# Expert weights in 2 MB loads of 16 KB per partition, in a transformer-block kernel on one Trainium2 core

## The chip, the core and the metric

The kernel runs on one core of a Trainium2 chip. Its engines are TensorE (PE; PEld is its weight load), VectorE (DVE), ScalarE (ACT), GpSimd (POOL) and SyncE (SP), which issues nearly all DMAs; 16 DMA engines carry the bytes. Each engine runs its own instructions in the order in which they stand, and a semaphore holds an instruction back until what it needs is there. The metric is the time of one execution on the device, in microseconds (us): the median of three runs before the change is 1225.87 us.

## What is computed

One layer on 256 tokens of width 1024, float32, with 16 meta tokens ahead of them. The first part mixes a gated attention branch and a state-space (S5) branch; the second part is a mixture of 32 experts, and all 32 experts' weights are read:

```python
h = layer_norm(concat([meta, x]), ln_in_g, ln_in_b)
proj = h @ w_in                      # q, k, v, forget gate, u, and two gates g_a, g_b
y_a = forgetting_attention(q, k, v, log_f)
y_b = gelu(s5_ssm(u, ...)); y_b = y_b * sigmoid(y_b @ w_glu + b_glu)
mix = (sigmoid(g_a) * (y_a @ w_up_a) + sigmoid(g_b) * (y_b @ w_up_b)) @ w_o
h = layer_norm(ALPHA * h + mix, ln1_g, ln1_b)
top_v, top_i = top_k(h @ w_router + b_router, 4); top_w = softmax(top_v)
for e in range(32):
    gate = minimum(h @ w_gate[e] + b_gate[e], 7); up = clip(h @ w_up[e] + b_up[e], -7, 7)
    out += comb[:, e] * (((up + 1) * gate * sigmoid(1.702 * gate)) @ w_down[e] + b_down[e])
h = layer_norm(ALPHA * h + out, ln2_g, ln2_b)
```

Each expert has three matrices of 1024 x 1024 float32, 4 MB each: 384 MB in all.

## The kernel before

**Slots.** Weights live in slots of 8 KB per partition (1 MB over 128 partitions). Three pools hold them: `wA` (6 slots, open from the start), `wC` (5, in memory that the attention part frees) and `wB` (7, in memory that the scan part frees). Three tiles of the same size serve as further slots when their first use is over: `gate1` and `acc` in the pool `keep`, `hT` in `fk`. In the first part `wA` takes the slabs of `w_in`, `w_up_a`, `w_glu` and `w_up_b` (`slab`), two slots to a slab, and `wB` the four quarters of `w_o`.

**Expert loads.** `expert_load(w, e, qtr)` loads a quarter of an expert's matrix, 256 rows: partition p gets the rows 2p and 2p+1, so that one run of 8192 bytes goes to a partition. `home` lists the slot of each load in order: 21 loads find a slot without waiting for an expert (`first`); after that the slots come round again, 20 of them, later 19. `prefetch` issues the first 21 loads between the steps of the first part, in the order gate, up of expert 0, gate, up of expert 1, then down.

**Order.** SP and PE run in the order in which the code is written (`manual_schedule`); in most of the kernel the instructions of DVE, ACT and POOL are put in an order by a list scheduler, which moves an instruction ahead where its inputs are expected early. SP's DMAs use eight semaphores in turn, so an issue also waits until the DMA eight places earlier has landed, and everything behind a waiting issue waits with it.

**First part.** `u_tile`, `k_tile`, `q_tile`, `v_tile` and `gate_tile` are projections on PE (`project`, L214). Between them stand the scan (`scan_b`, `scan_u`, `scan_out`), whose tables `E` DVE builds by doubling (L419 to L422), and the attention (`scores`, `values`). `wr` (router weights) and `brow` are loaded behind the slab `wv`; from them POOL makes `wrg` (L675, L677) and DVE reduces `wsum` (L676, L678, L679). `braw` holds the gate and up biases; ACT casts it to `bias` (L834, L838), and POOL subtracts in between (L837).

**Experts.** The 32 experts run in pairs p. `gate_up` multiplies the pair's gathered tokens (64 per expert) with gate and up, two matmuls of 512 columns for each of the eight k, `activate` and `act_T` make and transpose the activations, `gather` collects the next pair's tokens, and `down` goes through the down matrices of both experts together. The last pair is taken expert by expert (`down_one`). As a partition holds the rows 2p and 2p+1, k stands for every second column within 256: `paired(k)` takes these columns of `z1` and of the activations, and `affine` the matching norm parameters from `pcolP`.

Of the kernel before, what the change touches and what calls it, by code (L numbers as in the profile page):

```python
# [33 lines left out]
NWA, NWB, NWC = 6, 7, 5  # L34
# [14 lines left out]
def hybrid_trunk_kernel(ctx: ExitStack, tc: tile.TileContext, x, meta, ln_in_g, ln_in_b, w_in, b_f,  # L49
# [44 lines left out]
    prowP = sp.tile([8, 256], F32, name="prowP")  # L94
    ldt = sp.tile([16, 2], F32, name="ldt")

    def slab(src, kt):

        n = src.shape[1]
        src = src.rearrange("(k p) n -> p k n", p=P)  # L100
        nk, ks = 2048 // n, []
        for k0 in range(0, kt, nk):
            v_ = wA.tile([P, 2048], F32, name="w", tag="w").rearrange("p (k n) -> p k n", n=n)
            nc.sync.dma_start(v_, src[:, k0:k0 + nk])
            ks += [v_[:, k] for k in range(nk)]
        return ks
# [21 lines left out]
    for j, a in enumerate((ln1_g, ln1_b)):  # L128
        nc.sync.dma_start(prowP[4 * j:4 * j + 4], a.rearrange("l (q n) -> (l q) n", n=256))
# [140 lines left out]
    for k in range(2):  # L270
        TE.transpose(pp[:, 8 * k:8 * k + 8], prowP[:, k::2], ident[:8, :8])
# [424 lines left out]
    slots = [("wC", "w")] * NWC + [("wB", "w")] * (NWB - 4) + [("wA", "w")] * NWA + [("keep", "gate1")]  # L696
    slots += [("wB", "w")] * 4 + [("fk", "hT")]
    first = slots[:NWC + NWB + NWA - 3] + [("keep", "acc")] + slots[NWC + NWB + NWA - 3:]

    def homes():  # L700

        out = list(first)
        while len(out) <= 12 * NE:
            out += [s_ for s_ in slots if s_ != ("keep", "gate1") or len(out) < 9 * NE - 24]
        return out[:12 * NE + 1]
# [14 lines left out]
    def expert_load(w, e, qtr, load=True):  # L720
        key = (w.tensor.name, e, qtr)
        if key in ready:
            return ready.pop(key)
        pool, tag = home[nload[0]]
        nload[0] += 1
        t_ = pools[pool].tile([P, 2048], F32, name="w", tag=tag).rearrange("p (k n) -> p k n", n=D)
        if load:
            nc.sync.dma_start(t_, w[0, e, qtr * 256:qtr * 256 + 256].rearrange("(p k) n -> p k n", k=2))
        return t_

    def prefetch(n):
        seq = [(w, e, qtr) for e in range(2) for w in (w_gate, w_up) for qtr in range(4)]
        seq += [(w_down, e, qtr) for qtr in range(4) for e in range(2)]
        for _ in range(n):
            w, e, qtr = seq[nload[0]]
            ready[(w.tensor.name, e, qtr)] = expert_load(w, e, qtr)

    prefetch(2)
# [20 lines left out]
    prefetch(2)  # L759
# [39 lines left out]
    prefetch(NWB - 4)  # L799
# [74 lines left out]
    def paired(k):  # L874

        return slice(256 * (k // 2) + k % 2, 256 * (k // 2) + 256, 2)

    def affine(k, out_, in_, natural=False):
        if natural:
            g_, b_ = col(R_L1G + k), col(R_L1B + k)  # L880
        else:
            c = 8 * (k % 2) + k // 2
            g_, b_ = pcolP[:, c:c + 1], pcolP[:, c + 4:c + 5]
# [471 lines left out]
```

## Time and profile before

| | before |
|---|---|
| runs, median (lowest to highest) | 1225.87 us (1224.28 to 1227.44) |
| the profiled execution: its time, and the span from first to last instruction | 1222.52 us, 1221.0 us |
| busy: PE, PEld, DVE, ACT, POOL | 1124.1, 588.9, 340.4, 177.3, 71.6 us |
| DMA | 433.60 MB in 75674 packets, 355 GB/s over the span |
| chain of work that ended last | DMA 53%, PE 38%, DVE 5% |

PE's busy time counts pipelined matmuls whose ends are modelled, so 92% doesn't mean that PE sets the time. The chain is followed back from the last instruction; where it reads DMA, an instruction was waiting for a load. The trace gives, for each engine, every instruction with its start and duration and what ended its idle time, and for the DMA engines bytes, packets and the share of time in which they were busy.

### The profile page before, as it was taken

The page shows a single profiled execution, that of the slowest core. Times are in us where ns is not written, and L with a number is a line of the kernel's source. Part 1 is how long each engine was busy: PE and PEld are TensorE (multiplying, and loading weights), DVE is VectorE, ACT ScalarE, POOL GpSimd, SP SyncE. Part 2 cuts the span into 40 slices and gives each one's busy share as a digit, 9 for nine tenths or more (in the row PEclk, how much of TensorE's full clock was granted, in tenths as well). Part 3 has the DMA queues.
Part 4 walks back from the last instruction along what each step waited for, and adds up shares of the span by engine and source line. Part 5 has one row for each costly group of instructions (what it writes and reads, how often), then busy time and mean ns, then how long its engine had stood idle before and what let it go on. Part 6 is the DMA issues. An engine that isn't in the chain of part 4 may idle for free.

```text
span 1221.0 us, 13200 instructions
## 1 busy us (share of the span) xinstructions
PE 1124.1 (92%) x5398; PEld 588.9 (48%) x5399; DVE 340.4 (28%) x782; ACT 177.3 (15%) x387; POOL 71.6 (6%) x118
## 2 busy tenths in 40 slices
PE   4889999998999999999999999998999899998994
PEld 2777788754545444444434363535433343443331
DVE  3969420533221212112131312130212121202013
ACT  2357410311101011010101010101010111101000
POOL 3333200400000000000000000000000000000001
PEclk9999999998999999999999999999999999999998
DMA  7742289557999999999999999999999999999992
GB/s 150 187 105 69 104 211 357 221 208 301 413 422 420 423 420 421 422 420 407 421 422 422 421 422 421 421 421 419 422 420 422 421 421 421 421 421 420 422 421 104
DMA packets 75674, 433.60 MB, mean 355 GB/s; under 512 B 14218, under 2 KB 14570, under 8 KB 26586
## 3 DMA queue, kind: packets, MB, share of 16 engines
q1 hardware_dynamic: 75178, 432.19, 89.3%
q8 instruction: 44, 0.72, 0.2%
q10 hardware_dynamic: 432, 0.52, 0.1%
q14 instruction: 20, 0.16, 0.0%
HBM read 431.64 MB, written 1.05 MB: 354 GB/s over the span
## 4 chain that ended last, share of the span: by engine, by line
DMA 53%; PE 38%; DVE 5%; ACT 1%; issue 1%; POOL 1%; SPq 1%; POOLq 0%; ACTq 0%; DVEq 0%
DMA w<-in_w_up_dram 29%; DMA w<-in_w_down_dram 16%; PE ps L214 7%; PE pu L1062 6%; PE pg L1062 6%; PE Yp L1094 5%; DMA w<-in_w_gate_dram 5%; PE ps L764 2%; PE px L945 2%; DMA w<-in_b_down_dram 2%; PE Yp L1108 1%; PE ps L936 1%; PE po L936 1%; PE px L1124 1%; DMA prow<-in_ssm_a_im_dram 1%
## 5 line engine op out<-in xcount | busy, mean ns | idle before, releaser
L1062 PE MATMUL pu<-w,xy 128*64 128x512 f32 x1024 | 238.5, 595 | 13.5 <-DMA w<-in_w_up_dram 13.5
L1062 PE MATMUL pg<-w,xy 128*64 128x512 f32 x1024 | 236.9, 594 | 3.3 <-PEq L1153 2.1
L1094 PE MATMUL Yp<-w,aT 128*64 128x512 f32 x960 | 228.1, 611 | 0.0
L1094 PEld LDWEIGHTS Yp<-w,aT 128*64 128x64 f32 x960 | 101.5, 141 | 114.7 <-issue 99.1
L1062 PEld LDWEIGHTS pu<-w,xy 128*64 128x64 f32 x1024 | 81.4, 136 | 154.8 <-issue 108.9
L1062 PEld LDWEIGHTS pg<-w,xy 128*64 128x64 f32 x1024 | 86.6, 137 | 140.4 <-issue 134.0
L214 PE MATMUL ps<-hT,w 128*128 128x256 f32 (+1 forms) x512 | 119.3, 392 | 2.8 <-ACT pr L595 2.8
L214 PEld LDWEIGHTS ps<-hT,w 128*128 128x128 f32 x512 | 98.0, 194 | 19.7 <-ACT pr L595 3.1
L1072 DVE TENSOR_SCALAR pg<-pg 128x512 f32<-128x512 f32 x32 | 22.4, 699 | 232.7 <-PE pg L1065 232.7
L1073 ACT ACTIVATE ups<-pg 128x512 f32<-128x512 f32 x32 | 19.1, 597 | 415.3 <-DVE pg L1072 415.3
L1075 DVE TENSOR_SCALAR pu<-pu 128x512 f32<-128x512 f32 x32 | 22.4, 700 | 186.8 <-PE pu L1065 186.8
L1097 DVE COPY xy<-Yp 128x512 f32<-128x512 f32 x15 | 10.4, 692 | 223.3 <-PE Yp L1094 223.3
L1124 PE MATMUL px<-xy,selT 128*128 128x512 f32 x120 | 61.7, 636 | 4.7 <-DVE acc L1126 2.6
L945 PE MATMUL px<-sel,z 128*128 128x128 f32 x480 | 59.8, 283 | 0.6 <-DVE sel L950 0.6
L1313 POOL TENSOR_TENSOR acc<-acc,gb 128x512 f32<-128x512 f32 (+1 forms) x2 | 2.4, 1214 | 979.6 <-ACT acc L1311 979.6
L945 PEld LDWEIGHTS px<-sel,z 128*128 128x128 f32 x480 | 58.6, 196 | 0.8 <-ACT aT L1084 0.8
L1124 PEld LDWEIGHTS px<-xy,selT 128*128 128x128 f32 x120 | 20.4, 193 | 42.3 <-DVE acc L1126 19.2
L1126 DVE TENSOR_TENSOR acc<-acc,px 128x512 f32<-128x512 f32 x56 | 37.3, 683 | 12.3 <-PE px L1124 12.2
L1098 ACT COPY xy<-Yp 128x512 f32<-128x512 f32 x15 | 8.8, 586 | 218.3 <-PE Yp L1094 218.3
L1084 ACT COPY aT<-px 128x512 f32<-128x512 f32 x32 | 18.8, 586 | 133.6 <-PE px L1082 133.6
L885 DVE TENSOR_SCALAR xy<-px,pcolP 128x128 f32<-128x128 f32 x60 | 23.7, 410 | 45.4 <-ACT xy L887 43.4
L887 ACT ACTIVATE xy<-px,pcolP 128x128 f32<-128x128 f32 x60 | 25.8, 455 | 44.6 <-PE px L945 42.6
(399 smaller groups left out, 838.2 us busy)
## 6 DMA issues: line engine op xcount, KB each, us to landing
w<-in_w_gate_dram SPq DMA_DIRECT2D x128, 1024.0 KB
w<-in_w_up_dram SPq DMA_DIRECT2D x128, 1024.0 KB
w<-in_w_down_dram SPq DMA_DIRECT2D x127, 1024.0 KB
w<-in_w_in_dram SPq DMA_DIRECT2D x16, 1024.0 KB
w<-in_w_o_dram SPq DMA_DIRECT2D x4, 1024.0 KB
w<-in_w_up_a_dram SPq DMA_DIRECT2D x2, 1024.0 KB
w<-in_w_up_b_dram SPq DMA_DIRECT2D x2, 1024.0 KB
w<-in_w_glu_dram SPq DMA_DIRECT2D x1, 1024.0 KB
```

The source lines that it names most:

```text
L214: TE.matmul(pt, w[k][:, j * P:(j + 1) * P], hT[:, k, n0:n1], start=k == 0, stop=k == KD - 1)
L764: TE.matmul(pt, w[k][:, d * P:(d + 1) * P], y[:, k], start=k == 0, stop=k == 3)
L885: V.tensor_scalar(out_, in_, g_, b_, op0=ALU.mult, op1=ALU.add)
L887: S.activation(out_, in_, AF.Identity, scale=g_, bias=b_)
L936: TE.matmul(po[i][n], mT[:, k, i * P:(i + 1) * P], wo[k // 2][:, k % 2, n * 512:n * 512 + 512], start=False, stop=k == KD - 1, skip_group_ ...
L945: TE.matmul(pts[k // 4][:, (k % 4) * P:(k % 4 + 1) * P], z1[:, i, paired(k)], sel[:, i].rearrange("p e s -> p (e s)"), start=i == 0 and k ...
L1062: TE.matmul(pt[64 * n:64 * n + 64], XT[:, kk, c0:c0 + CAP], wt[:, k, n * 512:n * 512 + 512], start=kk == 0, stop=False, skip_group_check=True)
L1072: V.tensor_scalar_min(pgt, pgt, 7.0)
L1075: V.tensor_scalar(put, put, 7.0, -7.0, op0=ALU.min, op1=ALU.max)
L1094: TE.matmul(Yp[n][64 * g:64 * g + 64], aTs[g][:, j, half], wd[g][:, k, n * 512:n * 512 + 512], start=qtr == 0 and k == 0, stop=qtr == 3 an ...
L1124: TE.matmul(pt, selT[:, i * P:(i + 1) * P], Ysb[:, ns], start=True, stop=True)
L1126: V.tensor_add(acc[:, i, ns], acc[:, i, ns], pt)
```

## The change

An expert load is now half a matrix, 512 rows or 2 MB: partition p gets four neighbouring rows, 4p to 4p+3, one run of 16384 bytes. The slots are 16 KB per partition: 4 in `wA`, 3 in `wB`, 2 in `wC`. A load into the small tiles takes two of them (`PAIR`: `gate1` and `hT`; in the first round `acc` and `gate1`) and is issued as two DMAs of 1 MB. The first round has 10 loads (20 MB); after that the places come round, 10 of them, later 9. The slabs of the first part use the same slots, one slab to a slot, still in DMAs of 1 MB. The very last load is issued in two DMAs. `paired(k)` now steps by four columns, `prowP` has four rows and shares the tile `etmp` of the scan tables, and `down` goes through a half of each expert at a time. `crowded` handles the case that an expert has more than 64 tokens.

```diff
-NWA, NWB, NWC = 6, 7, 5
+NWA, NWB, NWC = 4, 3, 2
...
-    prowP = sp.tile([8, 256], F32, name="prowP")
+    prowP = sp.tile([P, 512], F32, name="prowP", tag="etmp")[:4]
...
-        nk, ks = 2048 // n, []
+        nk = 2048 // n
+        v_ = wA.tile([P, 4096], F32, name="w", tag="w").rearrange("p (k n) -> p k n", n=n)
         for k0 in range(0, kt, nk):
-            v_ = wA.tile([P, 2048], F32, name="w", tag="w").rearrange("p (k n) -> p k n", n=n)
-            nc.sync.dma_start(v_, src[:, k0:k0 + nk])
-            ks += [v_[:, k] for k in range(nk)]
-        return ks
+            nc.sync.dma_start(v_[:, k0:k0 + nk], src[:, k0:k0 + nk])
+        return [v_[:, k] for k in range(kt)]
...
-    slots = [("wC", "w")] * NWC + [("wB", "w")] * (NWB - 4) + [("wA", "w")] * NWA + [("keep", "gate1")]
-    slots += [("wB", "w")] * 4 + [("fk", "hT")]
-    first = slots[:NWC + NWB + NWA - 3] + [("keep", "acc")] + slots[NWC + NWB + NWA - 3:]
+    PAIR = (("keep", "gate1"), ("fk", "hT"))
+    slots = [(("wC", "w"),)] * NWC + [(("wB", "w"),)] * (NWB - 2) + [(("wA", "w"),)] * NWA + [PAIR]
+    slots += [(("wB", "w"),)] * 2
+    first = slots[:NWC + NWB + NWA - 2] + [(("keep", "acc"), ("keep", "gate1"))] + slots[-2:]
...
+    def part_load(t_, w, e, hf_, k0, nk):
+        nc.sync.dma_start(t_, w[0, e, 512 * hf_:512 * hf_ + 512].rearrange("(p k) n -> p k n", k=4)[:, k0:k0 + nk])
...
+        place = home[nload[0]]
         nload[0] += 1
+        ks = []
+        for pool, tag in place:
+            n = 4 // len(place)
+            t_ = pools[pool].tile([P, n * D], F32, name="w", tag=tag).rearrange("p (k n) -> p k n", n=D)
+            for k0 in range(0, n, nk):
+                part_load(t_[:, k0:k0 + min(n, nk)], w, e, hf_, len(ks) + k0, min(n, nk))
+            ks += [t_[:, k] for k in range(n)]
+        return ks
...
-    prefetch(2)
+    prefetch(1)
...
-    prefetch(NWB - 4)
+    prefetch(NWB - 2)
...
-        return slice(256 * (k // 2) + k % 2, 256 * (k // 2) + 256, 2)
+        return slice(512 * (k // 4) + k % 4, 512 * (k // 4) + 512, 4)
...
-        for qtr in range(4):
-            wd = [expert_load(w_down, 2 * p + g, qtr) for g in range(2)]
-            for k, n in ((0, 0), (0, 1), (1, 0), (1, 1)):
-                half, j = qtr // 2, 2 * (qtr % 2) + k
-                for g in range(2):
-                    TE.matmul(Yp[n][64 * g:64 * g + 64], aTs[g][:, j, half],
...
+        for hf_ in range(2):
+            wd = [expert_load(w_down, 2 * p + g, hf_) for g in range(2)]
+            for k in range(4):
+                for n in range(2):
+                    for g in range(2):
+                        TE.matmul(Yp[n][64 * g:64 * g + 64], aTs[g][:, k, hf_],
```

Line numbers after the change differ by one (first part) to eight. Three places at which the order of the instructions differs follow; the names are the program's tiles.

DVE and POOL in the first part, where DVE has finished the table of angles `ew` and goes on to `lr`, `zi` and the scan tables `E`; first DVE before, then DVE after:

```order
L350 SCALAR_TENSOR_TENSOR ew<-sn,cs 128x144
L358 TENSOR_TENSOR lr<-mag,ew 128x16
L361 TENSOR_TENSOR zi<-mag,ew 128x16
L424 COPY E_488<-ew 128x32
L359 TENSOR_SCALAR zr<-lr 128x16
L367 TENSOR_TENSOR t_419<-zi,pcol 128x16
```

```order
L349 SCALAR_TENSOR_TENSOR ew<-sn,cs 128x144
L675 TENSOR_REDUCE wsum<-wrg 128x32
L357 TENSOR_TENSOR lr<-mag,ew 128x16
L360 TENSOR_TENSOR zi<-mag,ew 128x16
L423 COPY E_487<-ew 128x32
L678 TENSOR_TENSOR wsum<-wsum,brow 1x32
L358 TENSOR_SCALAR zr<-lr 128x16
```

Then POOL at the same place, before and after (`wfp` is the forget gate's weight, `cL` a scan matrix):

```order
L277 TENSOR_SCALAR wfp<-wf 128x8x8 x4
L623 MEMSET vmz 128x512
L406 TENSOR_TENSOR cL_478<-cT_458,lr 128x512
L406 TENSOR_TENSOR cL_479<-cT_459,lr 128x512
L407 TENSOR_TENSOR q_480<-cT_459,zi 128x512
```

```order
L276 TENSOR_SCALAR wfp<-wf 128x8x8 x4
L622 MEMSET vmz 128x512
L674 TENSOR_TENSOR wrg<-wr,pcol 128x256
L676 TENSOR_TENSOR wrg<-wr,pcol 128x256
L405 TENSOR_TENSOR cL_477<-cT_457,lr 128x512
L405 TENSOR_TENSOR cL_478<-cT_458,lr 128x512
```

The products and sums of the router weights moved from behind the scan matrices and tables to ahead of them, on both engines.

ACT at the end of the first part (`gate` is the second gate, `tg` the gate of the S5 branch, `bias` the cast of `braw`), before and after:

```order
L744 ACTIVATE gate_1418<-ps 128x256 x8
L808 ACTIVATE tg<-ps,bh 128x256
L834 CAST bias<-braw 96x2048
L808 ACTIVATE tg<-ps,bh 128x256 x3
L838 CAST bias<-braw 32x2048 x3
```

```order
L750 ACTIVATE gate_1412<-ps 128x256 x6
L842 CAST bias<-braw 96x2048
L750 ACTIVATE gate_1412<-ps 128x256 x2
L846 CAST bias<-braw 32x2048
L816 ACTIVATE tg<-ps,bh 128x256 x2
L846 CAST bias<-braw 32x2048
```

The first cast moved ahead of the last two gate tiles.

SP's queue around the start of the experts (`cnti` is read into a register between two loads of `w_down`), before and after:

```order
L728 DMA w<-in_w_up_dram 128x2048
L728 DMA w<-in_w_gate_dram 128x2048 x4
L728 DMA w<-in_w_up_dram 128x2048 x4
L728 DMA w<-in_w_down_dram 128x2048 x5
L1152 TENSOR_LOAD cnti
```

```order
L712 DMA w<-in_w_up_dram 128x4096
L712 DMA w<-in_w_gate_dram 128x4096 x2
L712 DMA w<-in_w_up_dram 128x4096
L712 DMA w<-in_w_up_dram 128x2048 x2
L712 DMA w<-in_w_down_dram 128x4096 x2
L1159 TENSOR_LOAD cnti
```

Ahead of the register's load five quarters of `w_down` stood before, and two halves now.

## Rows read from the trace of the kernel before

**Rows 1.** The page: what the DMA engines moved, in 40 equal slices.

```profile
GB/s 150 187 105 69 104 211 357 221 208 301 413 422 420 423 420 421 422 420 407 421 422 422 421 422 421 421 421 419 422 420 422 421 421 421 421 421 420 422 421 104
```

**Rows 2.** The chain of waits in order of time: start us, us, what.

```profile
283.75 7.26 PE pg L1062 x32
...
335.36 6.34 PE pg L1062 x30
...
389.87 6.29 PE pg L1062 x30
...
1159.42 1.94 PE pu L1062 x8
```

**Rows 3.** Busy time by stretch: stretch, its us, five engines, PE clock, DMA share, GB/s.

```profile
184.00:190.00 6.00, 6.00 (x30) 5.28 (x29) 0.84 (x2) 0.38 (x1) 0.00 (x0) 1.00 1.02 418
243.00:249.00 6.00, 6.00 (x16) 2.65 (x15) 0.00 (x0) 0.00 (x0) 0.00 (x0) 1.00 1.01 425
...
450.00:1150.00 700.00, 661.61 (x3085) 298.40 (x3082) 143.97 (x245) 63.28 (x125) 0.00 (x0) 0.99 1.01 420
```

**Rows 4.** DMA queues, 450 to 1150 us: packets by size.

```profile
DMA packets 40403, 294.25 MB, mean 420 GB/s; under 512 B 4497, under 2 KB 4497, under 8 KB 4529
```

**Rows 5.** DMA queues, 46 to 56 us, in 40 slices of 0.25 us, and its packets.

```profile
GB/s 8 0 0 0 0 41 98 139 205 172 197 295 311 303 229 344 369 377 336 270 311 369 377 311 303 319 311 336 254 360 360 373 376 312 231 156 104 42 13 8
DMA packets 2100, 2.23 MB, mean 223 GB/s; under 512 B 1075, under 2 KB 1075, under 8 KB 2100
```

**Rows 6.** Timeline of SP's queue: start us, us, line, what it issues, count.

```profile
46.40 2.20 SPq L104 DMA_DIRECT2D w<-in_w_in_dram  x2
48.65 0.50 SPq L567 DMA_DIRECT2D wr<-in_w_router_dram  x1
```

**Rows 7.** Timeline of DVE, with idle time before and its releaser.

```profile
42.77 0.16 DVE L358 TENSOR_TENSOR lr<-mag,ew 128x16 f32<-128x16 f32 x1
...
60.11 0.43 DVE L536 SCALAR_TENSOR_TENSOR fa<-fx 128x272 f32<-128x272 f32 x1
...
61.72 0.59 DVE L676 TENSOR_REDUCE wsum<-wrg 128x32 f32<-128x256 f32 x1 [0.51 <-POOL wrg L675]
```

**Rows 8.** Timeline of POOL.

```profile
62.40 0.62 POOL L677 TENSOR_TENSOR wrg<-wr,pcol 128x256 f32<-128x256 f32 x1 [0.71 <-DVE wsum L676]
```

**Rows 9.** Timeline of ACT.

```profile
60.57 0.43 ACT L537 ACTIVATE fa<-fa 128x272 f32<-128x272 f32 x1 [5.90 <-DVE fa L536]
...
73.47 0.38 ACT L555 ACTIVATE qA<-ps 64x256 f32<-64x256 f32 x1 [1.72 <-PE ps L214]
...
74.27 0.59 ACT L462 COPY bT<-ps 128x512 f32<-128x512 f32 x1
...
216.65 1.90 ACT L834 CAST bias<-braw 96x2048 bf16<-96x2048 f32 x1 [0.97 <-DMA braw<-in_b_up_dram]
```

**Rows 10.** Timeline of PE in the first part.

```profile
51.70 21.74 PE L214 MATMUL ps<-hT,w 128*128 128x272 f32 x96
...
74.91 1.19 PE L481 MATMUL pb<-ux,bT 128*128 128x136 f32 x8 [0.78 <-ACT bT L462]
...
227.28 13.22 PE L764 MATMUL ps<-ya__1272,w 128*128 128x256 f32 x60 [2.54 <-DVE ya__1272 L809]
```

**Rows 11.** Timeline of SP's queue around the first expert.

```profile
272.65 0.80 SPq L728 DMA_DIRECT2D w<-in_w_down_dram  x2
285.90 3.76 SPq L728 DMA_DIRECT2D w<-in_w_down_dram  x3
```

**Rows 12.** Timeline of PE: the last load of `w_up` of expert 30.

```profile
1159.42 1.94 PE L1062 MATMUL pu<-w,xy 128*64 128x512 f32 x8 [0.55 <-DMA w<-in_w_up_dram]
```

**Rows 13.** Weight loads by line and form: count, busy us, mean ns, idle before.

```profile
L945 PEld LDWEIGHTS px<-sel,z 128*128 128x128 f32 x480 | 58.6, 196 | 0.8 <-ACT aT L1084 0.8
...
L1082 PEld LDWEIGHTS px<-ident,ups 128*128 128x128 f32 x128 | 17.8, 207 | 17.9 <-issue 9.6 <-DVE xy L885 5.4 <-DVE ups L1076 2.2
...
L818 PEld LDWEIGHTS po<-ident,hT 128*128 128x128 f32 x16 | 1.9, 192 | 0.1
```

More of the change, by code (lines that the diff above doesn't have):

```diff
@@ L269, in hybrid_trunk_kernel @@
     pp = pst(16)
-    for k in range(2):
-        TE.transpose(pp[:, 8 * k:8 * k + 8], prowP[:, k::2], ident[:8, :8])
+    for k in range(4):
+        TE.transpose(pp[:, 4 * k:4 * k + 4], prowP[:, k::4], ident[:4, :4])
     S.copy(pcolP, pp)
@@ L731, in prefetch @@
+        return ks
     def prefetch(n):
[L732 to L733 removed]
+        seq = [(w, e, hf_) for e in range(2) for w in (w_gate, w_up) for hf_ in range(2)]
+        seq += [(w_down, e, hf_) for hf_ in range(2) for e in range(2)]
         for _ in range(n):
[L735 to L736 removed]
@@ L881, in affine @@
         else:
[L882 to L883 removed]
+            c = 4 * (k % 4) + k // 4
+            g_, b_ = pcolP[:, c:c + 1], pcolP[:, c + 2:c + 3]
         if k % 2:
@@ L1102, in down_one @@
         Y = py_.tile([P, 512], F32, name="Yp", tag=f"Yp{e % 2}")
-        for qtr in range(4):
-            wd = expert_load(w_down, e, qtr)
-            for k in range(2):
-                half, j = qtr // 2, 2 * (qtr % 2) + k
+        for hf_ in range(2):
+            wd = expert_load(w_down, e, hf_)
+            for k in range(4):
                 for n in range(2):
-                    TE.matmul(Y[64 * n:64 * n + 64], aT[:, j, half], wd[:, k, n * 512:n * 512 + 512],
-                              start=qtr == 0 and k == 0, stop=qtr == 3 and k == 1, skip_group_check=True)
+                    TE.matmul(Y[64 * n:64 * n + 64], aT[:, k, hf_], wd[k][:, n * 512:n * 512 + 512],
+                              start=hf_ == 0 and k == 0, stop=hf_ == 1 and k == 3, skip_group_check=True)
         return Y
@@ L1154, in crowded @@
             free = list(slots)
-            for s_ in home[nload[0] - 8:nload[0]]:
+            for s_ in home[nload[0] - 4:nload[0]]:
                 free.remove(s_)
-            free = [s_ for s_ in free if s_[0] != "keep"]
-            free.sort(key=lambda s_: ("wC", "fk", "wB", "wA").index(s_[0]))
+            free = [s_[0] for s_ in free if s_ != PAIR]
             def slot(n):
                 pool, tag = free[n]
-                return pools[pool].tile([P, 2048], F32, name="w", tag=tag)
-            h1Td = slot(0).rearrange("p (k t) -> p k t", k=KD)
+                return pools[pool].tile([P, 4096], F32, name="w", tag=tag)
+            both = slot(0)
+            h1Td = both[:, :2048].rearrange("p (k t) -> p k t", k=KD)
             for k in range(KD):
@@ L1184, in crowded @@
                     nc.gpsimd.dma_start(bu, b_up[0, bass.ds(e, 1), :])
-                    aT = slot(2).rearrange("p (k t) -> p k t", k=KD)
-                    wg_e, wu_e = weights_of(w_gate, 3), weights_of(w_up, 7)
+                    if len(free) > 5:
+                        aT = slot(5)[:, :2048]
+                    else:
+                        aT = fk.tile([P, 2048], F32, name="w", tag="hT")
+                    aT = aT.rearrange("p (k t) -> p k t", k=KD)
+                    tg_, tu_ = ([slot(n + hf_).rearrange("p (k n) -> p k n", n=D) for hf_ in range(2)] for n in (1, 3))
+                    wg_e, wu_e = weights_of(w_gate, tg_), weights_of(w_up, tu_)
                     for i in range(2):
@@ L1260, in hybrid_trunk_kernel @@
     upB = activate(1, *gate_up(e + 1, lambda: combine_one(0, selT, False)))
-    for qtr in range(3):
-        ready[w_down.tensor.name, e + 1, qtr] = expert_load(w_down, e + 1, qtr)
-    last = expert_load(w_down, e + 1, 3, load=False)
-    for k in range(2):
-        part_load(last, w_down, e + 1, 3, k)
-    ready[w_down.tensor.name, e + 1, 3] = last
+    for hf_ in range(2):
+        ready[w_down.tensor.name, e + 1, hf_] = expert_load(w_down, e + 1, hf_, 4 - 2 * hf_)
     order.close()
```

78 lines of the change are left out of this document (37 added, 41 removed).

## Prediction, made before the changed kernel was run

> **What bounds the kernel now.** I read the page's row of bytes first, then the chain of waits, then stretches of the trace. The row of bytes [rows 1] has two regimes: up to about 300 us between 69 and 357 GB/s, then 420 almost without a gap. The chain [rows 2] agrees: the first pair of experts starts on PE at 283.75 us, pair after pair follows, and at 1159.42 an up matmul still waits for its load, 0.55 us [rows 12]; behind it stand 1221.0 - 1159.4 = 61.6 us of PE's own work. Over 450 to 1150 us the DMA engines are busy all the time (share 1.01) at 420 GB/s [rows 3].
>
> So the end is a sum of three: the start of the experts (a chain of computing), the loads at the DMA's rate, PE's tail. Check: 384 MB less 21 prefetched less some 15 that land behind the last awaited one are 348 MB (1 MB is 1048576 bytes); at 420 GB/s one takes 2.496 us, together 868.6 us; from the first load behind the start, 285.90 [rows 11], that is 1154.5, and the awaited load is used 4.9 us later, which the wait for a first free slot and the landing explain. PE has room: a pair takes it 389.87 - 335.36 = 54.5 us [rows 2], and the DMA 24 x 2.496 = 59.9. Between 283.75 and 1159.42 lie 875.7 us, PE's work there is 51.6 (first pair) + 14 x 54.5 + 14.5 (two groups of 7.26) = 829, so its slack is some 47 us.
>
> **Part 1, the descriptors: -9.6 us.** Near 186 us the DMA moves descriptors of 4 KB at 418 GB/s, near 246 us of 8 KB at 425 [rows 3]. With 16 engines a packet takes 156.8 ns and 308.4 ns. The second 4 KB thus cost 151.6, and 156.8 - 151.6 = 5.2 ns are fixed for a packet. Among the experts a packet of 8 KB takes 312 ns: 16 x 700 us over 40403 - 4497 = 35906 of them [rows 4]; the 4497 small ones are the semaphores, one to eight packets. One packet of 16 KB for two saves 5.2 of 624 ns, 0.8%. If the 3.6 ns between 312 and 308.4 hang on packets and semaphores too, both of which halve, it saves up to 2.0%. From the other side: nothing, if 8 KB already has all there is; and a loss as large as the nearest step the other way gained, 0.6%, can't be excluded, since no row has a run of 16 KB. I take 1.1%, nearer to the lower gain because the two measured sizes carry it: 0.011 x 868.6 = 9.6 us. Ends: -18 and +5.
>
> The Trainium skill ("DMA: Bandwidth & Descriptors", section "Why small descriptors are slow (HBM only)") gives a fixed overhead of about 3 cycles of the internal bus to a packet, against 512 cycles for 16 KB at 32 bytes each; that is less than the 5.2 ns that the rows give. By the page alone the gain would be 0.6%, an estimate of 5 us, and the whole sum 4.6 us later than mine.
>
> **Part 2, the first part: +8.1 us.** The diff doesn't show this; the order does. POOL now has `wrg` ahead of the scan matrices `cL`, and DVE has the first `wsum` ahead of `lr`, `zi` and the tables `E`. Both need `wr`, which is issued behind the slab `wv`, the last part of 6 MB of `w_in`. In the kernel before SP issued `wv` at 46.40 (it had waited for the slots of `wu`) and `wr` at 48.65 [rows 6]; the 128-byte pieces of `wr` then lie behind the slab in the queues, and the last bytes land near 55.6 us [rows 5]. The gap in those slices (nothing for 0.75 us, then a ramp) goes, since `wv` has a slot of its own now; I put `wr` at 54.0. DVE gets there at 42.77 us [rows 7]. It then waits until 54.0 + 0.1 + 0.62 for POOL's product [rows 8] and has 0.59 of its own [rows 7]: `lr` starts at 55.3 instead of 42.8, 12.5 us late. A smaller sum on one partition moves ahead too, and some 1.2 us of router work no longer stand later, so at `fa`, before at 60.11, about 12.0 remain. ACT's `exp` waited for exactly this `fa`, 5.90 us [rows 9], so it shifts in full. From there the chain goes over `bT` to PE: ACT had 1.72 us of waiting for PE at `qA`, which absorb as much; `bT` at 74.27 [rows 9] comes 10.3 us late, PE waited 0.78 for it at 74.91 [rows 10], so `pb` comes 10.3 late, and all behind it, since PE's 96 projections ahead of it [rows 10] stand still and have nothing to pull forward. No load is awaited between there and 195 us, so nothing gives the shift back.
>
> One thing does, later. Before, ACT's cast of `braw` waited for a DMA, 0.97 us, and took 1.90 [rows 9] ahead of the last `tg`, and PE then waited 2.54 us for `ya` [rows 10]. `braw` is queued behind slabs that need not wait for slots any longer, so it is there in time for the shifted chain, and the cast stands ahead of the last gate tiles. I give back 2.2 of the 2.54. Sum: 10.3 - 2.2 = +8.1; ends -2.2 (no wait at all) and +10.5 (`wr` at 55.6, only 1.4 given back).
>
> **Part 3, the slots: +6.0 us.** 20 MB are prefetched instead of 21: one more at 2.5 us. The first slot comes free after 16 row blocks on PE instead of 8. A block is two matmuls, and 32 of these take 7.26 us [rows 2], so half a matrix takes 3.6 and a quarter 1.8: +1.8. At the far end 16 blocks instead of 8 are left on PE when the last awaited load lands; its 8 matmuls take 1.94 [rows 12], so +1.7 to 1.9. SP's issues halve in number; its engine isn't the bound, [rows 11] show issues that wait for slots. In the first pair PE waits for loads at places a half apart; before, the three quarters of `w_down` at 285.90 were queued for 3.76 us [rows 11], after, halves for about as long: zero, between -1.5 and +3.
>
> **Part 4, every fourth column: +0.5 us.** Weight loads that take every second column last 196 ns (`z`) and 207 (`ups`) against 192 for neighbouring columns [rows 13], so a step costs at most 4 to 15 ns. On the path are 32 of the first gather and 8 in the tail; elsewhere PE's slack covers them (15 pairs of 40 loads at 15 ns are 9 of 47 us). Between 0 and 2.1 I take 0.5. `prowP` in the tile of the scan tables and the double-sized places of `PAIR` hang on nothing late: zero.
>
> **Sum:** -9.6 + 8.1 + 6.0 + 0.5 = +5.0 us. Against the profiled execution, 1222.52 us (span 1221.0), that is 1227.5; the median of the runs shown is 3.35 above it, and so **1230.9 us**, slower by 0.4%. A measurement tells about 0.3%, 3.7 us, from no change.
>
> **Rivals.** *A, the router's loads cost nothing.* If `wr` is there when DVE arrives near 43 us, part 2 is only the 2.2 given back. Each us that `wr` lands behind 43 counts in full, beyond the 1.7 that ACT has to spare; below 44.5 or so the change is not slower. For it speaks that slabs no longer wait for slots; against it that 6 MB at the rates of [rows 1] don't fit ahead of 44, and that in [rows 5] the small pieces run only late in the stretch. Then 1225.87 - 2.2 + 6.0 + 0.5 - 9.6 = 1220.6. *B, 16 KB bring nothing:* the engines are at share 1.01 already, and the rate of 420 may be set by memory and not by packets. Then parts 2 to 4 stand alone: 1225.87 + 14.6 = 1240.5. For it speaks that 8 KB gave only 1.7% over 4 KB [rows 3]; against it that all of this fits a fixed time per packet. *C, the column step makes PE the bound:* from 47 us / (15 x 40 loads) = 78 ns more per load PE has no slack left. If a step of four doubled a load's 196 ns, 600 x 196 ns = 118 us, less 47, and part 2 to 3 on top without the DMA's gain: about 1305. [Rows 13] show that the step of two costs a tenth of this at most.
>
> By the Trainium skill ("SBUF — State Buffer", section "Door 1: The DMA port swizzle (why `[64,N]` ≈ `[32,N]`)") memory lines are 16 bytes and full bandwidth wants two hits to a line; four float32 apart there is one hit per line, two apart there are two. That is rival C; the small cost at the step of two agrees with the rule, and no row here shows a step of four.
>
> **How the numbers follow.** Forecast 0.64, its own range 1224 to 1237 (descriptors between 0.6 and 1.6%, `wr` between 52 and 56): faster 0.04 of it, same 0.21, slower 0.39. A 0.16: faster 0.13, same 0.03. B 0.13 and C 0.04: slower. The rest, 0.03, evenly. Faster 0.18, same 0.25, slower 0.57. The range 1218 to 1241 takes in A and the middle of B; outside are C, the upper half of B, the lower edge of A and the rest, some 0.17.
>
> **What would show it.** Descriptors right: 424 or 425 GB/s over 450 to 1150 us instead of 420; wrong: 420 or less. Router wait right: DVE idle 11 to 12 us just ahead of the first `wsum`, released by POOL, which waits for `wr`; `pb` near 85 us and the first pair near 291; wrong (A): the pair at 281 to 284. Slots: the first load of `w_down` behind the start 3.6 us after it, not 2; the last wait on `w_up` 63 us before the end. Columns: mean of the weight loads of `z` under 215 ns; at 275 or more it is C. The forecast fails if PE, waiting for nothing, sets the time in the middle, or if stalls in the first pair come to over 5 us.

## The result, and the profile of the changed kernel

| | before | after |
|---|---|---|
| median (lowest to highest), us | 1226.01 (1224.28 to 1227.44) | 1295.40 (1293.23 to 1299.48) |
| ratio, 95% interval | | 1.0571 (1.0541 to 1.0600) |
| profiled span, us | 1221.0 | 1293.5 |
| first gate matmul of pair 0 / of the last expert | 283.75 / 1177.7 | 298.47 / 1250.6 |
| mean granted clock of TensorE | 0.984 | 0.969 |

The change made the kernel 69.4 us slower, 5.7%; 1230.9 had been forecast, 1218 to 1241 as the range. Of the 72.5 us between the two spans 14.7 arise before the first pair and 58.1 between the first pair and the last expert; the tail is about as long as before (43.0 and 43.3 us).

The page of the changed kernel, granted clock, DMA share (tenths) and bytes in 40 slices of 32.3 us:

```profile
PEclk9989999998999999999999898999999999999998
DMA  7830269447899999999587959999999999999980
GB/s 147 235 66 1 112 215 380 184 174 294 345 430 416 429 427 428 426 414 423 229 363 294 421 223 418 397 429 426 412 429 427 426 429 427 428 427 428 429 368 32
```

Where the row of before stood at some 420 almost without a gap [rows 1], this one reaches 427 to 430 and has holes: 229, 363, 294 and 223 between 614 and 776 us. The DMA has become faster and idles. The same in stretches (us, five engines, granted clock, DMA share, GB/s), to hold against [rows 3]:

```profile
300.00:450.00 150.00, 146.03 (x649) 67.27 (x645) 29.15 (x49) 14.20 (x27) 0.00 (x0) 0.98 0.95 397
450.00:620.00 170.00, 164.74 (x731) 79.43 (x732) 32.18 (x55) 14.57 (x29) 0.00 (x0) 1.00 1.01 424
620.00:800.00 180.00, 160.06 (x686) 74.55 (x684) 34.35 (x59) 14.56 (x29) 0.00 (x0) 0.94 0.76 316
800.00:1150.00 350.00, 335.23 (x1455) 163.42 (x1453) 69.45 (x119) 31.47 (x62) 0.00 (x0) 0.97 1.00 423
```

The page's summary of the chain of waits, by engine; before, its first entry was DMA with 53%:

```profile
PE 26%; DVE 2%; ACT 0%; POOL 0%; issue 0%; POOLq 0%; ACTq 0%
```

The chain reaches back only to about 921 us, so it covers the last 28% of the span; there no load is in it any more, and PE sets the end. PE's waits cover the rest (who waited for what, total us, times, longest). Before, 27 waits for `w_up`, about two a pair, marked a steady DMA bound; after, three are left, and the other two rows are single long ones. First before, then after:

```profile
PE pu L1062 <- DMA w<-in_w_up_dram: 13.5, 27, 1.1
```

```profile
PE Yp L1102 <- DMA w<-in_w_down_dram: 6.6, 1, 6.6
...
PE pu L1070 <- DMA w<-in_w_up_dram: 3.8, 3, 2.1
PE pg L1070 <- DMA w<-in_w_gate_dram: 3.5, 1, 3.5
```

Three things stand out in the trace.

**PE, weight loads of `z`** (count, busy us, mean ns), by line and form:

```profile
L953 PEld LDWEIGHTS px<-sel,z 128*128 128x128 f32 x480 | 113.1, 329 | 0.8 <-ACT aT L1092 0.8
...
L1090 PEld LDWEIGHTS px<-ident,ups 128*128 128x128 f32 x128 | 18.7, 210 | 17.8 <-issue 9.6 <-DVE xy L893 5.3 <-DVE ups L1084 2.2
```

329 ns with every fourth column, where every second one took 196 [rows 13]; those of `ups`, with the same step, stay at 210, 3 more than before. PE's timeline shows what it is worth: a gather's 32 matmuls, first in the kernel before, then after.

```profile
313.99 4.01 PE L945 MATMUL px<-sel,z 128*128 128x128 f32 x32 [0.61 <-DVE sel L950]
```

```profile
328.54 7.70 PE L953 MATMUL px<-sel,z 128*128 128x128 f32 x32 [0.61 <-DVE sel L958]
```

That is 3.7 us a pair. A pair in which PE waits for nothing lasts 58.1 us instead of 54.5; the DMA at 428 GB/s needs 24 x 2.45 = 58.8.

**POOL, DVE and PE in the first part.** POOL stands 14.77 us for the router weights `wr`, DVE 11.82 us for POOL's product of them, and PE's `pb`, before at 74.91 [rows 10], comes at 86.03:

```profile
54.61 0.62 POOL L674 TENSOR_TENSOR wrg<-wr,pcol 128x256 f32<-128x256 f32 x1 [14.77 <-DMA wr<-in_w_router_dram]
```

```profile
43.13 0.30 DVE L349 SCALAR_TENSOR_TENSOR ew<-sn,cs 128x144 f32<-128x144 f32 x1
55.26 0.60 DVE L675 TENSOR_REDUCE wsum<-wrg 128x32 f32<-128x256 f32 x1 [11.82 <-POOL wrg L674]
```

```profile
82.27 0.32 PE L465 MATMUL ps<-cT,bz 128*32 128x32 f32 x8 [4.04 <-ACT kA L550]
86.03 2.18 PE L480 MATMUL pb<-ux,bT 128*128 128x136 f32 x8 [3.44 <-ACT bT L461]
...
239.94 5.23 PE L770 MATMUL ps<-ya__1268,w 128*128 128x256 f32 x23 [1.19 <-DVE ya__1268 L817]
```

The granted clock of TensorE falls behind these waits (stretch, its us, five engines, granted clock, DMA share, GB/s; first before, then after):

```profile
60.00:230.00 170.00, 162.21 (x982) 136.83 (x981) 82.53 (x185) 65.74 (x172) 43.17 (x65) 1.00 0.59 184
```

```profile
60.00:230.00 170.00, 156.58 (x916) 130.75 (x915) 85.30 (x218) 61.28 (x169) 43.48 (x70) 0.96 0.47 150
```

**SP's queue** (start, us, line, what it issues, count; the us hold the wait of the issues in a row). After the load of `b_down` at 559.32 single groups hold the queue for 36.61, 46.40 and 58.22 us, and behind each a burst of issues goes out at once:

```profile
559.32 0.34 SPq L718 DMA_DIRECT2D w<-in_b_down_dram  x1
...
613.80 36.61 SPq L712 DMA_DIRECT2D w<-in_w_up_dram  x2
650.46 1.47 SPq L712 DMA_DIRECT2D w<-in_w_gate_dram  x3
651.98 1.02 SPq L712 DMA_DIRECT2D w<-in_w_up_dram  x2
...
663.82 46.40 SPq L712 DMA_DIRECT2D w<-in_w_gate_dram  x2
...
717.24 58.22 SPq L712 DMA_DIRECT2D w<-in_w_down_dram  x4
```

PE uses `b_down` for the first time at 808 us and for the last at 872, when the next wait in the queue ends:

```profile
872.11 1.98 PE L1145 MATMUL px<-w,cbT 32*128 32x512 f32 x4 [0.63 <-DVE cbT L1141]
```

`b_down` is 128 KB, but it takes a place in the round of the slots like any load, here one of the four of `wA`, and keeps it for over 300 us. The four places of `wA` follow one another in the round. With three left, the fourth load of each round waits for the slot that the first of the same round has just filled, three loads earlier in PE's order. The times agree: the wait of 36.61 us ends at 650.4, about when PE has gone through the first half of pair 6's first gate (from 645.65 on), three loads ahead of the one that waits. All other slots come free meanwhile, and no issue reaches them, since SP goes through its queue in order. Before, by the same list of places, it was one of the seven slots of `wB`, which lie apart in a round of 20, and SP's groups behind it last no longer than their loads take (eight in 18.30 us from 561.10 on).

### The profile page after: what moved, and what is told of

Read it like the earlier page. It is cut to its first block, busy times and chain, and to the rows that moved or that the text cites. A ratio compares the mean times of both kernels' runs of the same rounds, so it can differ in the third digit from the quotient of the medians.

```text
span 1293.5 us, 12868 instructions
## 1 busy us (share of the span) xinstructions
PE 1190.0 (92%) x5400; PEld 641.8 (50%) x5401; DVE 336.5 (26%) x782; ACT 177.3 (14%) x387; POOL 71.9 (6%) x118
## 5 line engine op out<-in xcount | busy, mean ns | idle before, releaser
L1070 PE MATMUL pu<-w,xy 128*64 128x512 f32 x1024 | 235.5, 596 | 3.8 <-DMA w<-in_w_up_dram 3.8
L1102 PE MATMUL Yp<-w,aT 128*64 128x512 f32 x960 | 232.3, 621 | 6.6 <-DMA w<-in_w_down_dram 6.6
L1102 PEld LDWEIGHTS Yp<-w,aT 128*64 128x64 f32 x960 | 92.7, 144 | 135.1 <-issue 112.9
L1070 PEld LDWEIGHTS pg<-w,xy 128*64 128x64 f32 x1024 | 83.8, 138 | 147.2 <-issue 139.1
L1070 PEld LDWEIGHTS pu<-w,xy 128*64 128x64 f32 x1024 | 84.7, 138 | 137.7 <-issue 124.6
L213 PE MATMUL ps<-hT,w 128*128 128x256 f32 (+1 forms) x512 | 122.8, 399 | 4.3 <-ACT pr L594 2.4
L953 PE MATMUL px<-sel,z 128*128 128x128 f32 x480 | 114.3, 397 | 0.6 <-DVE sel L958 0.6
L953 PEld LDWEIGHTS px<-sel,z 128*128 128x128 f32 x480 | 113.1, 329 | 0.8 <-ACT aT L1092 0.8
L1319 POOL TENSOR_TENSOR acc<-acc,gb 128x512 f32<-128x512 f32 (+1 forms) x2 | 2.4, 1218 | 1046.1 <-ACT acc L1317 1046.1
```

The source lines that it names most:

```text
L213: TE.matmul(pt, w[k][:, j * P:(j + 1) * P], hT[:, k, n0:n1], start=k == 0, stop=k == KD - 1)
L953: TE.matmul(pts[k // 4][:, (k % 4) * P:(k % 4 + 1) * P], z1[:, i, paired(k)], sel[:, i].rearrange("p e s -> p (e s)"), start=i == 0 and k ...
L1070: TE.matmul(pt[64 * n:64 * n + 64], XT[:, kk, c0:c0 + CAP], wt[k][:, n * 512:n * 512 + 512], start=kk == 0, stop=False, skip_group_check=True)
L1102: TE.matmul(Yp[n][64 * g:64 * g + 64], aTs[g][:, k, hf_], wd[g][k][:, n * 512:n * 512 + 512], start=hf_ == 0 and k == 0, stop=hf_ == 1 and ...
```

## Experiments

The theory after reading the two traces: the 16 KB descriptors do what they are for, and three losses hide it: the columns of `z` (PE loses its slack), the parked slot (the DMA idles), the router's wait (a late start). The rivals: one of the three is the whole loss; or 16 KB bring nothing. "Mended" stands for the changed kernel with all three losses taken out; it is described further down.

| kernel | median, us | ratio to before (95%) |
|---|---|---|
| before, columns in steps of four | 1263.73 | 1.0312 (1.0239 to 1.0385) |
| after, neighbouring columns | 1247.84 | 1.0182 (1.0145 to 1.0220) |
| after, `b_down` loaded late | 1272.47 | 1.0383 (1.0345 to 1.0421) |
| after, router sums late | 1286.69 | 1.0499 (1.0404 to 1.0595) |
| all three mended | 1218.88 | 0.9948 (0.9930 to 0.9966) |
| mended, descriptors of 8 KB | 1230.50 | 1.0046 (1.0030 to 1.0062) |
| mended, `b_down` parked | 1237.04 | 1.0099 (1.0073 to 1.0124) |
| mended, router sums early | 1232.39 | 1.0048 (1.0024 to 1.0071) |
| mended, columns in steps of four | 1274.60 | 1.0395 (1.0366 to 1.0425) |

The first four were measured in one round, the last two in another, the rest in a third; the kernel before had medians of 1226.02, 1224.87 and 1225.56 us there, so a difference across rounds is uncertain by about 1 us. One more kernel, with the steps of z in turn (1277.88 us, a single run), is used for its weight loads alone.

And from PE's timelines, the first pair's start and the us from pair to pair:

| kernel | first pair | pairs 1 to 5 (mean) | pairs 6, 7, 8, 9 |
|---|---|---|---|
| before | 283.75 | 54.5 | 58.1, 60.6, 59.1, 63.4 |
| after | 298.47 | 58.2 | 64.1, 80.8, 65.9, 65.0 |
| before, steps of four | 286.51 | 59.6 | 61.3, 61.5, 64.2, 63.1 |
| after, `b_down` late | 298.17 | 58.2 | 63.4, 62.6, 63.6, 63.4 |
| all three mended | 283.51 | 54.4 | 58.7, 58.4, 59.2, 64.3 |

### The columns of z

In the kernel before, one line of the gathers:

```diff
-            TE.matmul(pts[k // 4][:, (k % 4) * P:(k % 4 + 1) * P], z1[:, i, paired(k)],
+            TE.matmul(pts[k // 4][:, (k % 4) * P:(k % 4 + 1) * P], z1[:, i, slice(512 * (k // 4) + k % 4, 512 * (k // 4) + 512, 4)],
```

> The kernel before, in which only the gathers read the columns of z in steps of four (its result is then not the layer's, since the wrong columns are gathered); slots, descriptors and order as before. Theory: z's weight loads rise from 196 to about 329 ns as in the changed kernel and a pair takes PE 58.1 instead of 54.5 us, but the DMA at 59.9 us a pair still sets the time, so only the first gather (32 loads) and the rest of the slack show: 1228 to 1240 us. Rival (the column step by itself is the whole loss): 1280 to 1300 us.

1263.73 us, +37.7. That is neither: far over the theory's 1228 to 1240, and short of the rival's 1280 to 1300. The DMA doesn't set the time there any more; over 450 to 1150 us it moves less than before [rows 3]:

```profile
450.00:1150.00 700.00, 677.34 (x2965) 320.50 (x2963) 139.18 (x236) 58.98 (x116) 0.00 (x0) 0.98 0.98 403
```

The theory held PE's slack to be 47 us, as the prediction did; it is much smaller. The pairs 1 to 5, from which the 54.5 us come, are the lightest. The pairs 6 to 9 carry `residual` and `down_bias`, pair 12 the rows of the last norm. The changed kernel with `b_down` loaded late shows them where PE sets the time throughout: 63.4, 62.6, 63.6, 63.4 and 63.8 us against 58.1, together 26 us more (a part of this is the clock, which was 0.95 to 0.97 in the pairs 6 to 9 and 1.00 in pair 5). So some 20 of the 47 were there. The trace of before gives less still: from the first pair to the last awaited load PE waits 14.3 us for loads in all:

```profile
PE pu L1062 <- DMA w<-in_w_up_dram: 13.5, 27, 1.1
...
PE pg L1062 <- DMA w<-in_w_gate_dram: 0.8, 2, 0.5
```

15 gathers at 3.7 us more, and the first at 2.1, don't fit in either.

The clock adds to it. In the kernel before it stays at full speed through the first gather behind the start and what follows; with the step of four it doesn't. The same 17 us, from some 3 us behind the gather's start on, first before, then with the step:

```profile
317.00:334.00 17.00, 15.44 (x76) 9.15 (x76) 2.35 (x6) 2.68 (x6) 0.00 (x0) 1.00 1.00 405
```

```profile
320.00:337.00 17.00, 15.60 (x60) 9.88 (x61) 2.43 (x6) 2.68 (x6) 0.00 (x0) 0.80 0.61 241
```

0.80 means that for part of the stretch 1.2 GHz were granted instead of 2.4. What went ahead was the gather with the slow loads, in which PE's array does half as much in its time, and a wait of 1.40 us for `xy` that both kernels have. This returns at most of the first pairs: they take 59.2 and 60.3 us in turn, where 58.1 is what the same work takes at full clock.

The gather alone doesn't bring it about, though. In the changed kernel, with the same slow loads, a later gather (it starts at 505.30) and what follows run at full clock, as does the whole stretch from 450 to 620 us shown above:

```profile
508.00:525.00 17.00, 15.44 (x70) 9.62 (x71) 2.37 (x6) 2.68 (x6) 0.00 (x0) 1.00 1.01 428
```

What decides between the two stays open.

In the changed kernel the same line the other way:

```diff
-            TE.matmul(pts[k // 4][:, (k % 4) * P:(k % 4 + 1) * P], z1[:, i, paired(k)],
+            TE.matmul(pts[k // 4][:, (k % 4) * P:(k % 4 + 1) * P], z1[:, i, k * P:(k + 1) * P],
```

> The changed kernel, in which only the gathers read neighbouring columns of z (again the wrong ones for the result). Theory: z's loads are back at about 192 ns, a pair takes PE 54.5 us where nothing waits; the late start (about 298 us) and the idle DMA between 620 and 800 us remain: 1245 to 1270 us. Rival (the columns are the whole loss): 1220 to 1235 us; rival (PE is not the bound anywhere): 1290 or more.

1247.84, within the theory's range: the columns cost 47.6 of the 69.4 us, and are not all of it.

Then the size of the step itself:

```diff
...
+            if st == 1:
+                TE.matmul(o_, z1[:, i, 0:128:1], m_, start=a_, stop=b_, skip_group_check=True)
+            elif st == 2:
+                TE.matmul(o_, z1[:, i, 0:256:2], m_, start=a_, stop=b_, skip_group_check=True)
...
-                gather_mm(pts, sel, i)
+                gather_mm(pts, sel, i, (1, 2, 3, 4, 5, 6, 8)[(p - 1) % 7])
```

> The changed kernel, in which the gathers of the pairs 1 to 15 read the columns of z in steps of 1, 2, 3, 4, 5, 6 and 8 in turn (wrong columns, the time of one weight load is what is looked at). Theory (a load slows where only one float32 of a line of 16 bytes is used): about 192 ns at one, 196 at two, between at three, 330 at four, and no more than that at 5, 6 and 8. Rival (cost grows with the stride): rising beyond four.

Groups of weight loads, one line of the kernel for each step (L956 is step 1, L958 step 2, L960 step 3, L962 step 4, L964 step 5, L966 step 6, L968 step 8):

```profile
L968 PEld LDWEIGHTS px<-sel,z 128*128 128x128 f32 x64 | 15.4, 335 | 0.0
L962 PEld LDWEIGHTS px<-sel,z 128*128 128x128 f32 x64 | 15.1, 329 | 0.0
L966 PEld LDWEIGHTS px<-sel,z 128*128 128x128 f32 x64 | 14.5, 318 | 0.0
L964 PEld LDWEIGHTS px<-sel,z 128*128 128x128 f32 x64 | 14.4, 316 | 0.0
L960 PEld LDWEIGHTS px<-sel,z 128*128 128x128 f32 x64 | 11.3, 261 | 0.0
L956 PEld LDWEIGHTS px<-sel,z 128*128 128x128 f32 x96 | 11.1, 192 | 0.9 <-ACT aT L1105 0.8
L958 PEld LDWEIGHTS px<-sel,z 128*128 128x128 f32 x64 | 7.8, 196 | 0.0
```

192 and 196 ns at one and two, 261 at three, 316 to 335 from four on: a threshold and then a plateau, not a cost that grows with the stride. It has the form of the rule in the Trainium skill ("SBUF — State Buffer", section "Door 1: The DMA port swizzle (why `[64,N]` ≈ `[32,N]`)"): lines of 16 bytes, full bandwidth from two hits to a line. By it two of four float32 are free, one of four is not, and beyond that it gets no worse; these loads agree. Those of the transposes go otherwise. With neighbouring columns a transpose's load takes 142 ns in the kernel before, for instance that of `sel`:

```profile
L1024 PEld LDWEIGHTS px<-ident,sel 128*128 128x128 f32 x32 | 3.3, 142 | 23.9 <-DVE xy L885 23.9
```

Those of `ups` take 207 ns with every second column [rows 13] and 210 with every fourth: whatever a step costs there, all of it is there at two. No run changes the step of `ups` alone, and why it differs stays open.

At the other end, in the mended kernel (below) the step of four alone:

```diff
-            TE.matmul(pts[k // 4][:, (k % 4) * P:(k % 4 + 1) * P], z1[:, i, k * P:(k + 1) * P],
+            TE.matmul(pts[k // 4][:, (k % 4) * P:(k % 4 + 1) * P], z1[:, i, paired(k)],
```

> The mended kernel, but the gathers read z in steps of four columns (the wrong ones in this kernel). Theory (a pair then takes PE 58.1 us where it waits for nothing, and the pairs 6 to 9 and 12 some 63, so that PE and no longer the DMA sets the time): no waits of PE for up loads in the middle, 1250 to 1265 us. Rival (the DMA's 58.8 us a pair still sets it, PE has some 40 us to spare): 1222 to 1235 us.

1274.60, 55.7 over the mended kernel and 10 over the theory's upper end. PE sets the time, as the theory said (it waits for no load there); the size left out the clock again: a mean of 0.964 against 0.984, and first pairs of 59.2 to 60.3 us instead of 58.1.

### The parked slot

```diff
...
-        if p == 5:
-            bdown = [load_rows(b_down[0])]
-        elif p in (6, 7):
+        if p in (6, 7):
             residual(p - 6)
         elif p in (8, 9):
+            bdown = [load_rows(b_down[0])]
             down_bias(p - 8)
```

> The changed kernel, in which b_down is loaded right ahead of each of its two uses instead of four pairs earlier, so that it doesn't hold one of the four slots of wA over these pairs. Theory (the parked slot makes the fourth load of a round wait for one only three places ahead): SP's waits of 37 to 58 us and the idle DMA between 620 and 800 us go, pairs 7 to 9 fall from 64, 81 and 66 us to about 60 to 62: 1268 to 1280 us. Rival (the DMA idles there because PE is late anyway): no change, 1290 to 1299.

1272.47, 22.9 less, within the theory's range. The long pairs (6 to 8 in the table, counted from 0) come down to 63.4, 62.6 and 63.6 us, a little less far than expected. In the stretch that had moved 316 GB/s at a share of 0.76:

```profile
620.00:800.00 180.00, 172.27 (x752) 89.09 (x750) 40.97 (x70) 14.53 (x29) 0.00 (x0) 0.97 0.97 408
```

and between 600 and 720 us, where SP had waited for 36.61, 46.40 and 58.22 us, its longest group is 8.00 us:

```profile
645.27 8.00 SPq L712 DMA_DIRECT2D w<-in_w_down_dram  x4
```

Behind each of the two late loads of `b_down` a shorter wait of some 20 us is left. PE's waits for loads, 13.9 us in the changed kernel, are gone altogether. The rest of the 22.9 us goes beside a higher clock, 0.97 here and 0.98 over 800 to 1150 us against 0.94 and 0.97; that the clock is its cause isn't shown by itself.

In the mended kernel, the same edit backwards:

> The mended kernel, but b_down is loaded four pairs ahead of its uses again and holds a slot of wA meanwhile. Theory: SP waits of 30 us and more between 560 and 870 us are back, the DMA idles, and as the DMA sets the time here the loss is not smaller than in the changed kernel: 15 to 35 us over the mended kernel. Rival (with PE at 54.5 us a pair it doesn't matter): within 5 us of it.

1237.04, 18.2 over the mended kernel: the loss is there without the columns too. Waits of SP and idle DMA are back:

```profile
626.05 42.94 SPq L719 DMA_DIRECT2D w<-in_w_gate_dram  x2
...
676.53 51.22 SPq L719 DMA_DIRECT2D w<-in_w_down_dram  x4
```

```profile
620.00:800.00 180.00, 156.55 (x714) 66.77 (x716) 41.06 (x68) 13.96 (x28) 0.00 (x0) 0.95 0.91 380
```

### The router's wait

`gmark` is POOL's last instruction on `cL`, `vmark` DVE's scan of the forget gate:

```diff
-    G.tensor_mul(wrg, wr, bc(col(R_L1B, KD), 2, NE))
+    with tc.issue_after(gmark.ins), tc.issue_after(vmark.ins):
+        G.tensor_mul(wrg, wr, bc(col(R_L1B, KD), 2, NE))
...
```

> The changed kernel, with the router products and sums kept behind the scan matrices on POOL and behind the forget gate's scan on DVE, about where they stood before. Theory (the wait of 11.8 us for the router weights shifts everything behind it): pb near 75 us, first pair at about 287 us, 1281 to 1288 us. Rival (the shift is taken up later): 1292 to 1299.

1286.69 from two runs that lie 9 us apart, 8.7 less than the changed kernel; the two intervals overlap, so this time by itself settles little. The mechanism is plain: `pb` is back at 74.91 us, and the first pair starts at 286.2 instead of 298.5. Of these 12.3 us a part was lost again behind it, where PE set the time; the mean clock of the profiled execution, the slower of the two, was 0.962 against 0.969. The clean measure is the mended kernel without this edit:

> The mended kernel, but the router's products and sums may again run ahead of the scan matrices and tables. Theory (the wait for the router weights shifts the start of the experts one for one, and as the DMA sets the time behind it, all of that remains): first pair 9 to 12 us later than in the mended kernel (283.5), 1226 to 1231 us. Rival (the shift is hidden by the loads prefetched meanwhile): within 3 us of the mended kernel's 1218.9.

1232.39, 13.5 more (12.3 by the two ratios to before); first pair at 298.35 against 283.51. Where the DMA sets the time, nearly all of a late start stays. The expectation ended at 1231, since it put the shift at 9 to 12 us; it is 14.8. PE's waits there are those of the changed kernel:

```profile
83.41 0.32 PE L465 MATMUL ps<-cT,bz 128*32 128x32 f32 x8 [4.04 <-ACT kA L550]
```

### All three mended, and what the descriptors bring

`z1` is stored with its columns in the order of the gathers (ACT writes it so when it copies it from PSUM), the router's weights are loaded in the same order of rows, DVE reads `z1` back in the natural order for the residual, and the two edits above are in:

```diff
...
-                S.copy(z1[:, i, n * 512:n * 512 + 512], po[i][n])
+                S.copy(z1[:, i, n * 512:n * 512 + 512].rearrange("p (k q) -> p q k", k=4),
+                       po[i][n].rearrange("p (q k) -> p q k", k=4))
...
-            TE.matmul(pts[k // 4][:, (k % 4) * P:(k % 4 + 1) * P], z1[:, i, paired(k)],
+            TE.matmul(pts[k // 4][:, (k % 4) * P:(k % 4 + 1) * P], z1[:, i, k * P:(k + 1) * P],
```

> The changed kernel with all three mended: z is stored with its columns in the order in which the gathers read them (neighbouring columns, the layer's result is kept; the router's weights are loaded in the same order of rows), b_down is loaded right ahead of its uses, the router's sums stay late. Theory (2 MB loads of 16 KB descriptors run at 428 instead of 420 GB/s, and the three losses hid that): first pair near 286 us, pairs of 58 to 60 us set by the DMA, 1208 to 1218 us, ahead of the kernel before by 0.7 to 1.5%. Rival (the 428 were only there because the DMA had pauses): no faster than before, 1224 or more.

1218.88 us, 0.52% ahead of the kernel before (0.34 to 0.70%) and 5.9% ahead of the changed one: it beats both, though it lies 0.9 us beyond the slow end of the theory's range. The DMA is the bound again, at 426 GB/s where 428 had been expected, and PE waits for `w_up` as it did before:

```profile
450.00:1150.00 700.00, 658.03 (x3101) 297.06 (x3098) 146.00 (x247) 63.90 (x126) 0.00 (x0) 0.99 1.01 426
```

```profile
PE pu L1080 <- DMA w<-in_w_up_dram: 14.5, 13, 2.0
```

Then the same slots, filled by two DMAs of 1 MB with descriptors of 8 KB:

```diff
-    def expert_load(w, e, hf_, nk=4):
+    def expert_load(w, e, hf_, nk=2):
```

> The mended kernel, with every expert load issued as two DMAs of 1 MB with descriptors of 8 KB into the same slots. Theory (the descriptor's size makes the rate): 420 GB/s over 450 to 1150 us and 12 to 17 us more than the mended kernel, 1222 to 1232 us. Rival (the slots or the order make the rate): the same time as the mended kernel within 3 us.

1230.50, 11.6 more, just under the theory's 12 to 17, and the rate falls to that of before:

```profile
450.00:1150.00 700.00, 651.69 (x3056) 276.25 (x3053) 144.13 (x244) 62.73 (x124) 0.00 (x0) 0.99 1.01 420
```

Nothing but the issues differs between the two, so the descriptor's size and the halved number of DMAs, which these runs don't separate, are worth 11.6 us together. What is left of the change comes to 1230.50 - 1225.56 = 4.9 us; the bigger slots are the largest part of it that the prediction counted, but no run takes them alone.

## Why the prediction was wrong

**The columns (part 4): the step that failed.** I took 0.5 us and an upper bound of 2.1 from rows that show a step of two: since that step costs 4 to 15 ns a load [rows 13], I took a step of four to cost about as much. It costs 133 ns more than a step of two, and over the kernel, against neighbouring columns, 47.6 us (taken out of the changed kernel) to 55.7 (put into the mended one). The cost has a threshold between the two (196, 261, 329 ns), and a row below it says nothing of what lies beyond. It was the one place where the trace of before couldn't give a bound, and I treated it as if it did. The 15 ns were a slip as well: they compare the transposes of `ups` (207 ns) with `hT` (192), which goes through a plain matmul; transposes of neighbouring columns took 142 ns in the same trace. What spoke against the change stood in the text as rival C, at 0.04 and about 1305 us (its own terms add up to 1311), with the rule of the Trainium skill ("SBUF — State Buffer", section "Door 1: The DMA port swizzle (why `[64,N]` ≈ `[32,N]`)") beside it; the run gave 1295.4, and the loads' 329 ns are over the 275 that had been named as C's sign. Its mechanism was right in the main: 512 loads at 133 ns more, of which 115 show on PE (7.70 - 4.01 us over 32), not 600 at 196.

**PE's slack (the bound): 47 us were some 20 or less.** I multiplied 54.5 us, read from early pairs, by 14; the pairs 6 to 9 and 12 take 26 us more in all. With 20 us, rival C's threshold of 78 ns for a load would have been 33. PE's waits for loads, 14.3 us in all, stood in the same trace and would have shown that 47 is too much.

**The slots (part 3): size right, one wait missed.** 6.0 us were forecast; 4.9 are left for the slots and all else that isn't in the other parts. The last wait for `w_up` was forecast 63 us before the end, and lies 64.6 before it in the mended kernel. But I looked at the slots only as a count of bytes. That a small load keeps a place from pair 5 to pair 9 was in the code and harmless at one of seven places apart; at one of four in a row it costs 18.2 to 22.9 us, a term that isn't in the sum at all. The places in the first pair were looked at, the order in which they come round later was not.

**The first part (part 2): mechanism right, size too small.** DVE's wait ahead of the first `wsum` was forecast as 11 to 12 us and is 11.82; `pb` was forecast near 85 us and came at 86.03. The give-back was put at 2.2 us and is 1.35 (2.54 [rows 10] to 1.19). Two things weren't in the forecast. PE loses another 2.9 us between `pb` and `ya`, where the clock is lower (0.96 against 1.00 over 60 to 230 us) behind its new waits of 4.04 and 3.44 us; and the slow loads of the first gather (3.77 and 4.08 us against 2.04 and 3.75) cost 2.1. So 11.1 + 2.9 - 1.35 + 2.1 make +14.7 instead of +8.1. By the run that puts this step alone back into the mended kernel it costs 13.5 us of time.

**The descriptors (part 1): right.** 9.6 us forecast, 11.6 measured; 424 to 425 GB/s forecast, 426 measured. The 5 us, an estimate from the figure of the Trainium skill alone ("DMA: Bandwidth & Descriptors", section "Why small descriptors are slow (HBM only)"), lie well under the 11.6. The end of +5 us rested on a step that gained 0.6%, which no row shows: from 4 to 8 KB they show 1.7%. Rival B (16 KB bring nothing) is out. Rival A fell with DVE's wait.

By the measured terms: -11.6 + 4.9 + 13.5 + 55.7 (columns) + 18.2 (parked slot) = 80.7, against the 69.4 measured. Each of the last three is the price of one fault in the mended kernel; together they overlap by some 11 us. That a PE which sets the time hides part of the DMA's pauses is the likely reason; no run shows it by itself.

## What to carry to other kernels

- A price from a row holds for the shape in that row. Where a change doubles a stride, look for the threshold between the two before putting it at the old price, above all on an engine whose slack is to hide it; and count that slack over all rounds of a loop, the heavy ones too, and hold it against the waits that the engine really has.
- When slots get fewer and bigger, go through what else lives in them and for how long: one long-lived tenant, however small, can turn a round of places into a queue that waits for its own newest entry, and everything behind that issue stands still.
- A compiled order can move work ahead of a load that hasn't landed. Where the order shows a new consumer of a load on an engine that feeds the chain, put its wait into the sum; here 13.5 of 14.8 us were paid at the end.

## What the runs showed of the hardware

- Weight loads of 128 columns float32 take 192 ns at step 1, 196 at 2, 261 at 3, 329 at 4, 316 at 5, 318 at 6 and 335 at 8. Those of transposes take 142 ns with neighbouring columns (`sel`) and 207 to 210 at steps two and four (`ups`); why these differ stays open.
- With all 16 DMA engines busy, runs of 16 KB move 426 GB/s and runs of 8 KB 420, in the same slots and the same order, over the same 700 us. In the kernel before, runs of 4 KB moved 418 near 186 us and runs of 8 KB 425 near 246 [rows 3], so the stretch counts as well as the size.
- Behind a gather with slow weight loads TensorE was granted 1.2 GHz for some us (0.80 as the mean of 17 us) at work that ran at 2.4 GHz before, and this came back at most of the first pairs; but in the changed kernel the same gathers went by at 1.00 from 450 to 620 us. So a price for slow loads that is read at full clock can be too low, and when it is stays open.
